# Eight tokens' gate one-hots per VectorE pass, 37 leading key rows and gate runs of 384 bytes in a product-key expert layer

## The chip, the cores and the metric

One NeuronCore of one Trainium2 chip runs the whole program. The metric is the device time of one execution in microseconds (us). The engines that matter here are TensorE (PE, with its weight loads PEld), VectorE (DVE), ScalarE (ACT), GpSimd (POOL) and SyncE (SP), which only issues DMAs here.

## What is computed

Two transformer blocks on 512 tokens of width 1024. The first mixes by a gated delta rule and a forgetting attention, with a SwiGLU layer; the second has a windowed attention, a short convolution and the layer that the change touches, `peer`. It picks for each token, by 8 heads, 16 of 16384 experts and adds up their outputs:

```python
def peer(h, wq, subkeys, u_tab, v_tab):
    q = (xt @ wq).reshape(T, PEER_HEADS, 2, PEER_HALF)
    sc = jnp.einsum('thpd,hpkd->thpk', q, subkeys)
    vals, ids = lax.top_k(sc, PEER_TOPK)
    cand = (vals[:, :, 0, :, None] + vals[:, :, 1, None, :]).reshape(T, PEER_HEADS, 256)
    cid = (ids[:, :, 0, :, None] * PEER_KEYS + ids[:, :, 1, None, :]).reshape(T, PEER_HEADS, 256)
    top, pos = lax.top_k(cand, PEER_TOPK)
    idx = jnp.take_along_axis(cid, pos, axis=-1)
    g = jax.nn.softmax(top, axis=-1)
    ...
        a = jnp.einsum('chkd,cd->chk', jnp.take(u_tab, ic, axis=0), xc)
        wgt = gc * jax.nn.gelu(a)
        return jnp.einsum('chk,chkd->cd', wgt, jnp.take(v_tab, ic, axis=0))
```

An expert's number is 128 times a first key (0 to 127) plus a second key (0 to 127).

## The kernel before

The tokens lie in four tiles of 128. For tiles 1 to 3 (384 tokens, `ND`) the layer is computed densely: all 16384 experts' products with the 384 tokens, times a gate that is zero for the experts not picked. For tile 0 the picked rows of the two tables are fetched by indirect DMAs (`gather`), multiplied on DVE, and added up.

**The dense part** goes by first keys r, 128 of them, each with 128 experts. `ustep` makes the 128x384 products of row r (24 matmuls with 384 columns: the fp32 operands are each split in a high and a low part, and three of the four products are taken, eight times over the width) and ACT writes their gelu into a ring of rows X (`xrow`). `vstep` multiplies a row by its gates (`gmul`), splits it (`eh` on ACT, `el` on DVE in `split`), and adds it times the second table into six PSUM banks (18 matmuls with 512 columns). The weights of either step come as 512 KB loads into three buffers `wraw` (`wdma`, on SP's queue) and are split into `whi` (ACT, L232) and `wlo` (DVE, L234 in this part).

**The gates** of the dense part form a 128x128 matrix for each token (first key by second key). `gates_of` makes it on PE: for a token, a one-hot of the second keys of its 128 picks (`o2`, 128 picks by 128 keys, in fp16) and a one-hot of the first keys scaled by the gate's high and low part (`wh`, `wl`), then two matmuls with 128 columns. Before the change it takes 4 tokens at a time: 12 DVE instructions with 128 columns (L1969 to L1971), then 8 matmuls into one PSUM bank (`sums`), one ACT pass (L1959) that writes it into the staging tile `sg` of 12 tokens (two buffers), and, when that is full, one DMA from ACT's queue (L1963) of 768 KB into the tensor G in HBM. The sums stand one step behind the one-hots. G is read back by first keys in groups of `GR` rows (`ring`, L1829, on SP's queue, two buffers `gt`).

**The order** is written by hand with generators. `chosen` (the top 16 of a tile's candidates and their keys, on DVE), `weigh` (the softmax) and `gates_of` yield costs; `tick(pace)`, called 8 times in a `ustep` and 8 times in a `vstep`, adds `pace` to an account and runs that work until the account is used up. So the pace sets how much gate work stands between two matmuls of a step. The stages of `peer` are:

1. The last scores' top 16 and the first `ustep`s.
2. `ustep`s up to row `LEAD`, with `chosen` and the gates of tiles 1 to 3 between their matmuls, at `PACE0`. What is left of that work is finished behind the last of these steps. X has NX1 + NX2 row slots, one more than LEAD.
3. Pairs of a `ustep` (row k + LEAD) and a `vstep` (row k): first with `chosen` of tile 0 (`PACE1`), then with the gather (`PACE2`).
4. `vstep`s alone, when all 128 products are made, with what is left of the gather (`PACE3`). `preload` fetches the residual rows into free slots of X, `finish` writes the result.

Of the kernel before, what the change touches and what calls it, by code (L numbers as in the profile page):

```python
# [10 lines left out]
F32 = mybir.dt.float32  # L11
F32R = mybir.dt.float32r
F16 = mybir.dt.float16
I32 = mybir.dt.int32
U32 = mybir.dt.uint32
AF = mybir.ActivationFunctionType
OP = mybir.AluOpType
# [12 lines left out]
ND = 384  # L30
TB = 12
NB = ND // TB
GR = 4
GS = 32768.0

NX1, NX2 = 30, 14
LEAD = 43
NLAST = 18

PACE0, PACE1, PACE2, PACE3 = 0.62, 0.27, 0.21, 0.15  # L40

C_ANW, C_FNW, C_GNW, C_CW, C_AOG, C_COG, C_CW2, C_CT, C_N1, C_N2, C_FIN, C_N = 0, 8, 16, 17, 65, 69, 73, 85, 93, 101, 109, 117
R_ALOG, R_DTB, R_FB, R_SNK, R_QG, R_KG, R_IF, R_N = 0, 4, 8, 16, 24, 88, 152, 184
# [85 lines left out]
class Kern:  # L129
# [1580 lines left out]
    def peer(self):  # L1710


        nc, tc, a = self.nc, self.tc, self.a
        V, S, G = nc.vector, nc.scalar, nc.gpsimd
        hi, lo = self.h2
        with ExitStack() as es:
            qp = es.enter_context(tc.tile_pool(name="qp", bufs=1))
            self.X = [self.tl(qp, [128, NX1, ND], F32)]
            hm = self.tl(qp, [128, D], F32)
            ga = self.tl(qp, [128, D], F32)  # L1720
            self.idx = self.tl(qp, [128, 128], I32)
            self.g0 = self.tl(qp, [128, 128], F32)
            av = self.tl(qp, [128, 128], F32)
            self.i1T, self.i2T, self.ghT, self.glT = [self.tl(qp, [128, ND], F32) for _ in range(4)]
            iota = self.tl(qp, [128, 128], F16)
            self.G = self.tl(self.dr, [128 // GR, 128, NB, GR, TB], F32)
            ub = [self.bank("gx") for _ in range(2)]
            with tc.tile_pool(name="q1", bufs=1, side="right") as q1:
                vals = self.tl(q1, [128, 4, 16, 16], F32)
                ids = self.tl(q1, [128, 4, 16, 16], U32)  # L1730
                with tc.tile_pool(name="q2", bufs=2, side="right") as q2:
                    sub = self.tl(q2, [128, 16, 128], F32, bufs=1)
                    nc.sync.dma_start(sub, a["sub"].rearrange("p (a k) -> p a k", a=16))

                    def second(f, qT):
                        p2 = self.bank("pj")
                        for t in range(4):
                            g = slice(t * 128, t * 128 + 128)
                            self.mm(p2[:, g], qT[:, g], sub[:, f])
                        sc = self.tl(q2, [128, 4, 128], F32, "sc")  # L1740
                        S.copy(sc, p2.rearrange("p (t k) -> p t k", t=4))
                        self.top16(*[[x[:, t] for t in range(4)] for x in (sc, vals[:, :, f], ids[:, :, f])])
                    pend = []
                    for f in range(16):
                        p = self.first[f][0] if f < 3 else self.proj512(hi, lo, 0)
                        qT = self.tl(q2, [128, T], F32, "qT", bufs=5)
                        S.copy(qT, p)
                        if f == 3:

                            for n in range(2):  # L1750
                                pb = self.bank("pj")
                                for j in range(4):
                                    k = n * 4 + j
                                    t0 = self.tl(q2, [128, 128], F32, "t0")
                                    V.tensor_tensor(t0, hi.bitcast(F32)[:, k, 0:128], lo.bitcast(F32)[:, k, 0:128], op=OP.add)
                                    self.tr(pb[:, j * 128:j * 128 + 128], t0)
                                S.copy(hm[:, n * 512:n * 512 + 512], pb)
                        pend.append((f, qT))
                        if f > 2:
                            second(*pend.pop(0))  # L1760
                        if f == 4:
                            self.topk_consts(q1, iota)
                    for n, x in enumerate(pend):
                        second(*x)
                        if n < len(pend) - 1:
                            self.ustep(hi, lo, n, ub)
                    r0 = len(pend) - 1
                xp = es.enter_context(tc.tile_pool(name="xp", bufs=1, reuse_waits="tile"))
                self.X.append(self.tl(xp, [128, NX2, ND], F32))
                self.due = 0.0  # L1770
                gp = tc.tile_pool(name="q3", bufs=1, side="right", reuse_waits="tile")
                q3 = gp.__enter__()
                work = self.choice(q1, q3, vals, ids, iota)

                def tick(pace):
                    self.due += pace
                    while self.due > 0:
                        c = next(work, None)
                        self.due = self.due - c if c else -1e9
                for r in range(r0, LEAD):  # L1780
                    self.ustep(hi, lo, r, ub, lambda: tick(PACE0))
                for _ in work:
                    pass
                gp.__exit__(None, None, None)
                self.due = 0.0

                rp = es.enter_context(tc.tile_pool(name="rp", bufs=2, reuse_waits="tile"))
                self.ring(rp, 0)
                last = self.chosen(q1, 0, vals[:, 0], ids[:, 0])
                vb = [self.bank("gx")] + [self.bank("pj") for _ in range(4)] + [self.bank("hold")]  # L1790
                gat = self.gather(qp, hm, ga, av)

                def rest():
                    yield from last
                    for x in self.late:
                        yield from x
                    self.chose0 = True
                    yield from gat
                work = rest()
                self.gmul(rp, 0)  # L1800
                self.split(rp, 0)

                k = 0
                self.chose0 = False
                while not self.chose0:
                    self.ustep(hi, lo, LEAD + k, ub, lambda: tick(PACE1))
                    self.vstep(rp, k, vb, lambda: tick(PACE1))
                    k += 1
            for k in range(k, 126):
                if k + LEAD < 128:  # L1810
                    self.ustep(hi, lo, LEAD + k, ub, lambda: tick(PACE2))
                pace = PACE2 if k + LEAD < 128 else PACE3
                self.vstep(rp, k, vb, lambda: tick(pace))
                if k == 128 - NLAST:
                    self.preload()
            for _ in work:
                pass
            self.finish(rp, ga, vb)
# [126 lines left out]
    def gates_of(self, q3, t, iota):  # L1945

        nc, V, S = self.nc, self.nc.vector, self.nc.scalar
        lag = []

        def sums(n, o2, wh, wl):  # L1950
# [10 lines left out]
            if q + 4 == TB:  # L1961
                b = n * 4 // TB
                nc.scalar.dma_start(self.G[:, :, b].rearrange("g p r t -> p g (r t)"),  # L1963
                                    self.stage.rearrange("p (g r) t -> p g (r t)", r=GR))
        for n in range((t - 1) * 32, t * 32):
            o2, wh, wl = [self.tl(q3, [128, 4, 128], F16, tag, bufs=2) for tag in ("o2", "wh", "wl")]
            for j in range(4):
                c = slice(n * 4 + j, n * 4 + j + 1)
                V.tensor_scalar(o2[:, j], iota, self.i2T[:, c], None, op0=OP.is_equal)  # L1969
                V.tensor_scalar(wh[:, j], iota, self.i1T[:, c], self.ghT[:, c], op0=OP.is_equal, op1=OP.mult)  # L1970
                V.tensor_scalar(wl[:, j], iota, self.i1T[:, c], self.glT[:, c], op0=OP.is_equal, op1=OP.mult)  # L1971
            lag.append((n, o2, wh, wl))
            yield 0.6
            if len(lag) > 1:
                sums(*lag.pop(0))
            yield 0.6
        sums(*lag.pop(0))

    def gather(self, qp, hm, ga, av):
        nc, a = self.nc, self.a  # L1980
# [142 lines left out]
    def weigh(self, q1, t, tv, i1, i2):  # L2123
        nc = self.nc
        V, S = nc.vector, nc.scalar
        tt = lambda shape, dt, tag, n=1: self.tl(q1, shape, dt, "c" + tag, bufs=n)
# [11 lines left out]
        o = slice((t - 1) * 128, t * 128)  # L2138
        pt = self.bank("pj")
        for n, v in enumerate((i1, i2, g)):  # L2140
            self.tr(pt[:, n * 128:n * 128 + 128], v)
        S.copy(self.i1T[:, o], pt[:, 0:128])
        S.copy(self.i2T[:, o], pt[:, 128:256])
        gh = tt([128, 128], F16, "gh")
        S.activation(gh, pt[:, 256:384], AF.Copy, scale=GS)
        S.copy(self.ghT[:, o], gh)
        V.scalar_tensor_tensor(self.glT[:, o], pt[:, 256:384], GS, gh, op0=OP.mult, op1=OP.subtract)
        yield 0.3


# [12 lines left out]
```

## Time and profile before

| | us |
|---|---|
| median of 3 runs | 2482.51 (2479.33 to 2485.78) |
| the profiled execution | 2484.06 |
| its span | 2482.2 |
| PE busy in the span | 2350.2 (95%) |
| DVE busy | 1746.3 (70%) |
| ACT busy | 899.8 (36%) |

The span runs from the first to the last instruction of the program; the profiled execution's own time is 1.9 us longer, and 1.55 us above the median. A row of the profile names a line of the kernel, an engine, an operation and the tiles (output <- inputs); a busy time is the sum of durations, and neighbouring instructions of one engine overlap a little, so that starts tell more than durations where instructions are short. `u` is the name of every tile without one: the rows X, the key tiles, the accumulator of the gather. [...]

### The profile page before, as it was taken

What the parts mean: (1) busy time and instruction counts of PE and PEld (TensorE: products, weight loads), DVE (VectorE), ACT (ScalarE), POOL (GpSimd) and SP (SyncE); (2) the same over time, 40 slices, a digit from 0 to 9 for tenths busy, and PEclk for the clock granted to TensorE, in tenths of its full rate; (3) what the DMA queues carried; (4) which work ended last, traced back from release to release, by engine and by line L of the source; (5) the groups of instructions that cost most, each with busy time, mean ns of one, the idle gap of its engine ahead of it and who ended that gap; (6) DMA issues with size and microseconds to landing.
All of it is one profiled execution on the core that took longest, in us unless ns stands there. A gap on an engine that the chain in (4) does not pass through costs nothing. (4 is left out here: it accounts for less than half of the span.)

```text
span 2482.2 us, 32865 instructions
## 1 busy us (share of the span) xinstructions
PE 2350.2 (95%) x12063; PEld 1978.1 (80%) x12063; DVE 1746.3 (70%) x3991; ACT 899.8 (36%) x1389; POOL 795.1 (32%) x519
## 2 busy tenths in 40 slices
PE   7898999999999999989888888899999999999998
PEld 7888778877778777778767666789999999998776
DVE  6875334465540356757999999677878887878776
ACT  4442423332222333343335454343333333333332
POOL 3553102455544443433000000033434343434221
PEclk9899878999999999999989888999999999999999
DMA  3122000365552221232256677589999899999885
GB/s 120 57 76 76 26 1 11 126 232 193 203 153 93 77 85 59 69 111 86 77 116 131 132 137 138 147 286 319 336 323 329 321 337 321 335 326 324 280 319 174
DMA packets 254493, 438.13 MB, mean 177 GB/s; under 512 B 155006, under 2 KB 155926, under 8 KB 254204
## 3 DMA queue, kind: packets, MB, share of 16 engines
q1 hardware_dynamic: 84476, 272.79, 31.7%
q0 software_dynamic: 37312, 135.20, 15.8%
q10 hardware_dynamic: 132544, 28.05, 7.0%
q8 instruction: 94, 1.54, 0.3%
q14 instruction: 67, 0.55, 0.1%
HBM read 405.22 MB, written 30.70 MB: 176 GB/s over the span
## 5 line engine op out<-in xcount | busy, mean ns | idle before, releaser
L232 ACT CAST whi<-wraw 128x1024 fp32r<-128x1024 f32 x400 | 418.7, 1048 | 327.3 <-issue 125.1
L234 POOL TENSOR_TENSOR wlo<-wraw,whi 128x1024 fp32r<-128x1024 f32 x135 | 353.0, 2616 | 381.9 <-ACT whi L232 377.7
L234 DVE TENSOR_TENSOR wlo<-wraw,whi 128x1024 fp32r<-128x1024 f32 x265 | 329.6, 1244 | 160.1 <-ACT whi L232 158.1
L1996 POOL DMA_INDIRECT gr<-in_pu_dram,u x128 | 153.3, 1198 | 673.4 <-DVE u L2119 447.2
L161 PE MATMUL gx<-alo,whi 128*128 128x384 f32 x1024 | 353.6, 345 | 0.0
L161 PE MATMUL gx<-ahi,whi 128*128 128x384 f32 x1024 | 353.6, 345 | 0.0
L161 PE MATMUL pj<-ahi,whi 128*128 128x512 f32 (+2 forms) x1000 | 322.2, 362 | 3.4 <-ACT ahi L339 3.1
L161 PE MATMUL pj<-alo,whi 128*128 128x512 f32 (+2 forms) x1000 | 314.3, 354 | 0.0
L1996 POOL DMA_INDIRECT gr<-in_pv_dram,u x128 | 152.1, 1188 | 279.4 <-DVE u L2015 209.9
L161 PE MATMUL gx<-ahi,wlo 128*128 128x384 f32 x1024 | 219.8, 355 | 11.8 <-DVE wlo L234 11.8
L161 PE MATMUL pj<-ahi,wlo 128*128 128x512 f32 (+2 forms) x1000 | 211.2, 355 | 2.2 <-DVE wlo L234 2.2
L161 PEld LDWEIGHTS pj<-ahi,whi 128*128 128x128 f32 x1000 | 176.5, 194 | 35.9 <-issue 7.5
L161 PEld LDWEIGHTS gx<-ahi,whi 128*128 128x128 f32 x1024 | 197.1, 192 | 7.7
L161 PEld LDWEIGHTS gx<-alo,whi 128*128 128x128 f32 x1024 | 196.9, 192 | 6.9
L161 PEld LDWEIGHTS gx<-ahi,wlo 128*128 128x128 f32 x1024 | 188.9, 199 | 16.8 <-DVE wlo L234 15.0
L161 PE MATMUL pj<-whi,eh 128*128 128x512 f32 x512 | 201.4, 393 | 0.0
L161 PE MATMUL pj<-wlo,eh 128*128 128x512 f32 x512 | 200.6, 392 | 0.0
L161 PEld LDWEIGHTS pj<-alo,whi 128*128 128x128 f32 x1000 | 176.0, 193 | 23.8
L161 PEld LDWEIGHTS pj<-ahi,wlo 128*128 128x128 f32 x1000 | 166.3, 193 | 29.0 <-DVE wlo L234 2.6
L161 PE MATMUL pj<-whi,el 128*128 128x512 f32 x512 | 180.1, 392 | 0.0
L1899 ACT ACTIVATE u<-gx 128x384 f32<-128x384 f32 x128 | 63.4, 495 | 302.2 <-PE gx L161 294.9
L2015 DVE SCALAR_TENSOR_TENSOR u<-gr,u,u 128x1024 f32<-128x1024 f32 x128 | 163.8, 1280 | 3.2 <-DMA gr<-in_pv_dram,u 2.4
(472 smaller groups left out, 4152.4 us busy)
## 6 DMA issues: line engine op xcount, KB each, us to landing
wraw<-in_put_dram SPq DMA_DIRECT2D x128, 512.0 KB
wraw<-in_pv_dram SPq DMA_DIRECT2D x128, 512.0 KB
nu<-in_adaw_dram SPq DMA_DIRECT2D x48, 512.0 KB
u<-sg ACTq DMA_DIRECT2D x32, 768.0 KB
gt<-u SPq DMA_DIRECT2D x32, 768.0 KB
wraw<-in_wgu_dram SPq DMA_DIRECT2D x44, 512.0 KB
wraw<-in_wi_dram SPq DMA_DIRECT2D x28, 512.0 KB
wraw<-in_wd_dram SPq DMA_DIRECT2D x22, 512.0 KB
```

What stands on the lines that cost most here:

```text
L161: self.nc.tensor.matmul(out, l, r, start=start, stop=stop)
L232: self.nc.scalar.copy(hi, raw)
L234: (self.nc.vector if i in self.lov else self.nc.gpsimd).tensor_tensor(lo, raw, hi.bitcast(F32), op=OP.subtract)
L1899: self.nc.scalar.activation(self.xrow(r), p, AF.Gelu_apprx_tanh)
L1996: G.indirect_dma_start(out=u, out_offset=None, in_=a[items[i][0]], in_offset=bass.IndirectOffsetOnAxis(ap=self.idx[:, items[i][1]:items[i] ...
L2015: V.scalar_tensor_tensor(ga, u, wv[:, s:s + 1], ga, op0=OP.mult, op1=OP.add)
```

## The change

`gates_of` takes 8 tokens at a time, with four DVE instructions of 1024 columns: both operands are tiles read with a broadcast. For that the keys and gates of the 384 tokens (`i1T`, `i2T`, `ghT`, `glT`) are kept as fp16, each value twice side by side, so that the innermost run of every operand is two neighbouring elements. `wh` is first the bare one-hot; `wl` is made from it, then it is scaled in place. The sums of the step before come in two halves. `GR` is 8: G is laid out in groups of 8 first keys, so a run in HBM has 8 x 12 x 4 = 384 bytes (192 before), and a read fetches 8 rows (1.5 MB). X has 38 slots and LEAD is 37. When the gates are done before row LEAD, the tiles of the later stages are opened there and the rest of the `ustep`s run with `chosen` of tile 0 at `PACE1`.

```diff
-GR = 4
+GR = 8
-NX1, NX2 = 30, 14
-LEAD = 43
-NLAST = 18
-PACE0, PACE1, PACE2, PACE3 = 0.62, 0.27, 0.21, 0.15
+NX1, NX2 = 30, 8
+LEAD = 37
+NLAST = 11
+PACE0, PACE1, PACE2, PACE3 = 0.85, 0.27, 0.21, 0.15
...
-            self.i1T, self.i2T, self.ghT, self.glT = [self.tl(qp, [128, ND], F32) for _ in range(4)]
+            self.i1T, self.i2T, self.ghT, self.glT = [self.tl(qp, [128, ND, 2], F16) for _ in range(4)]
...
                 for r in range(r0, LEAD):
-                    self.ustep(hi, lo, r, ub, lambda: tick(PACE0))
-                for _ in work:
-                    pass
-                gp.__exit__(None, None, None)
...
+                    self.ustep(hi, lo, r, ub, lambda: tick(PACE0 if not ready else PACE1))
+                    if r == LEAD - 1:
+                        for _ in range(0 if ready else 10**6):
+                            if next(work, None) is None:
+                                break
+                    if not ready and (self.due < -1e6 or r == LEAD - 1):
+                        ready = True
+                        gp.__exit__(None, None, None)
+                        self.due = 0.0
+                        rp = es.enter_context(tc.tile_pool(name="rp", bufs=2, reuse_waits="tile"))
+                        self.ring(rp, 0)
+                        gat = self.gather(qp, hm, ga, av)
...
+                        work = rest()
...
-            for j in range(4):
-                c = slice(n * 4 + j, n * 4 + j + 1)
-                V.tensor_scalar(o2[:, j], iota, self.i2T[:, c], None, op0=OP.is_equal)
-                V.tensor_scalar(wh[:, j], iota, self.i1T[:, c], self.ghT[:, c], op0=OP.is_equal, op1=OP.mult)
-                V.tensor_scalar(wl[:, j], iota, self.i1T[:, c], self.glT[:, c], op0=OP.is_equal, op1=OP.mult)
...
+            bt = lambda ap: ap[:, n * GT:n * GT + GT].unsqueeze(2).to_broadcast([128, GT, 64, 2])
+            V.tensor_tensor(v4(o2), b2, bt(self.i2T), op=OP.is_equal)
+            yield 0.66
+            V.tensor_tensor(v4(wh), b2, bt(self.i1T), op=OP.is_equal)
+            yield 0.66
+            V.tensor_tensor(v4(wl), v4(wh), bt(self.glT), op=OP.mult)
+            yield 0.66
+            V.tensor_tensor(v4(wh), v4(wh), bt(self.ghT), op=OP.mult)
             lag.append((n, o2, wh, wl))
...
+            for m in range(2 if len(lag) > 1 else 0):
+                sums(lag[0][0] * 2 + m, *[x[:, m * 4:m * 4 + 4] for x in lag[0][1:]])
```

On DVE, in the gates of tile 1 before the change (`o` is `o2`, 128x128 its size; `u_8624` and `u_8623` are the keys, `u_8625` and `u_8626` the gates' parts):

```order
L1969 TENSOR_SCALAR o_1840_10306<-u_8627,u_8624 128x128
L1970 TENSOR_SCALAR wh_10307<-u_8627,u_8623,u_8625 128x128
L1971 TENSOR_SCALAR wl_10308<-u_8627,u_8623,u_8626 128x128
L1969 TENSOR_SCALAR o_1845_10338<-u_8627,u_8624 128x128
L1970 TENSOR_SCALAR wh_10339<-u_8627,u_8623,u_8625 128x128
L1971 TENSOR_SCALAR wl_10340<-u_8627,u_8623,u_8626 128x128
```

And at that place after the change, with one split of weights (`wlo`) among three steps of 8 tokens:

```order
L1974 TENSOR_TENSOR o_1883_10511<-u_8627,u_8624 128x1024
L1976 TENSOR_TENSOR wh_10512<-u_8627,u_8623 128x1024
L234 TENSOR_TENSOR wlo_10522<-wraw_10320,whi_10520 128x1024
L1978 TENSOR_TENSOR wl_10513<-wh_10512,u_8626 128x1024
L1980 TENSOR_TENSOR wh_10512<-wh_10512,u_8625 128x1024
L1974 TENSOR_TENSOR o_1892_10559<-u_8627,u_8624 128x1024
L1976 TENSOR_TENSOR wh_10560<-u_8627,u_8623 128x1024
L1978 TENSOR_TENSOR wl_10561<-wh_10560,u_8626 128x1024
L1980 TENSOR_TENSOR wh_10560<-wh_10560,u_8625 128x1024
L1974 TENSOR_TENSOR o_1897_10596<-u_8627,u_8624 128x1024
```

Four long instructions stand where 24 short ones stood, and two of the four read what the one before them or the second before them wrote.

On ACT, at the end of the gates before the change (L1899 is the gelu that ends a `ustep`, L1836 the `eh` that begins a `vstep`):

```order
L1959 ACTIVATE sg_13618<-pj_13648 128x4x128
L1959 ACTIVATE sg_13618<-pj_13661 128x4x128
L1963 DMA u_8628<-sg_13618 128x32x48
L1899 ACTIVATE u_9635<-gx_8630 128x384
L232 CAST whi_13691<-wraw_13509 128x1024
L1899 ACTIVATE u_9635<-gx_8629 128x384
L1836 CAST eh_13735<-u_8617 128x384
```

And after it:

```order
L1962 ACTIVATE sg_12263<-pj_12275 128x4x128
L1966 DMA u_8628<-sg_12263 128x16x96
L1902 ACTIVATE u_9635<-gx_8629 128x384
L232 CAST whi_12308<-wraw_12115 128x1024
L1902 ACTIVATE u_9635<-gx_8630 128x384
L232 CAST whi_12352<-wraw_12230 128x1024
L1902 ACTIVATE u_9635<-gx_8629 128x384
L232 CAST whi_12405<-wraw_12312 128x1024
L1902 ACTIVATE u_9635<-gx_8630 128x384
L232 CAST whi_12436<-wraw_12356 128x1024
L1902 ACTIVATE u_9635<-gx_8629 128x384
L1839 CAST eh_12494<-u_8617 128x384
```

Two gelus stood between the last store of gates and the first `vstep`, now five do, and the stored pieces are 16 groups of 96 values in place of 32 of 48.

On SP, the first loads of gate rows before the change (`put` is the first table, `pv` the second):

```order
L221 DMA wraw_13643<-in_pv_dram 128x1024
L221 DMA wraw_13695<-in_put_dram 128x1024
L1829 DMA gt_13726<-u_8628 128x1536
L221 DMA wraw_13743<-in_pv_dram 128x1024
L221 DMA wraw_13792<-in_put_dram 128x1024
L221 DMA wraw_13838<-in_pv_dram 128x1024
L1829 DMA gt_13865<-u_8628 128x1536
```

And after it:

```order
L221 DMA wraw_12115<-in_put_dram 128x1024
L221 DMA wraw_12230<-in_put_dram 128x1024
L1832 DMA gt_12306<-u_8628 128x3072
L221 DMA wraw_12312<-in_put_dram 128x1024
L221 DMA wraw_12356<-in_put_dram 128x1024
L221 DMA wraw_12409<-in_pv_dram 128x1024
L221 DMA wraw_12440<-in_put_dram 128x1024
L221 DMA wraw_12502<-in_pv_dram 128x1024
L221 DMA wraw_12538<-in_put_dram 128x1024
L221 DMA wraw_12573<-in_pv_dram 128x1024
L1832 DMA gt_12600<-u_8628 128x3072
```

The first load of gate rows now stands ahead of weights of the first table, and each is twice as large.

## Rows read from the trace of the kernel before

**Rows 1.** Windows by stage: length, then PE, PEld, DVE, ACT, POOL busy, PEclk, DMA, GB/s.
```profile
1189.80:1263.60 73.80, 57.37 (x304) 54.15 (x302) 72.43 (x335) 22.12 (x33) 0.00 (x0) 0.95 0.26 86
1263.60:1351.70 88.10, 76.66 (x431) 55.78 (x431) 85.87 (x391) 44.46 (x47) 0.00 (x0) 0.87 0.69 133
1351.70:1381.70 30.00, 25.83 (x147) 25.02 (x146) 29.28 (x122) 16.36 (x23) 0.00 (x0) 1.00 0.42 102
1381.70:1560.40 178.70, 154.87 (x877) 112.22 (x878) 174.59 (x789) 89.31 (x97) 0.00 (x0) 0.89 0.78 140
...
1568.10:2279.30 711.20, 704.84 (x3553) 641.78 (x3553) 571.97 (x799) 252.87 (x349) 268.36 (x221) 1.00 0.87 312
2279.30:2482.20 202.90, 191.93 (x792) 145.16 (x790) 151.31 (x187) 63.93 (x88) 42.50 (x40) 1.00 0.76 263
```
**Rows 2.** Waits, 1263.6 to 1560.4: who waited for whom, us, times, longest.
```profile
PEld L161 <- DVE o L1969: 39.2, 138, 0.3
PE pj L161 <- DVE wh L1970: 38.9, 132, 5.4
```
**Rows 3.** Timeline of DVE in the gates: start, us, instruction; one token.
```profile
1382.34 0.25 DVE L1969 TENSOR_SCALAR o<-u,u 128x128 f16<-128x128 f16 x1
...
1382.94 0.25 DVE L1969 TENSOR_SCALAR o<-u,u 128x128 f16<-128x128 f16 x1
```
**Rows 4.** Timeline of DVE in chosen, fp16 tensor by tensor, then a weight split.
```profile
1257.70 1.22 DVE L2112 TENSOR_TENSOR ccmp<-cpos,u 128x2048 f16<-128x2048 f16 x1
1258.96 1.71 DVE L2089 TENSOR_TENSOR cmu<-ccmp,cdl 128x256 f16<-128x256 f16 x8
1260.70 1.47 DVE L2094 TENSOR_TENSOR cmu<-cmu 128x1024 f16<-128x1024 f16 x3
1262.21 0.29 DVE L2096 TENSOR_TENSOR ci<-cmu 128x128 f32<-128x128 f16 x1
1262.42 1.22 DVE L234 TENSOR_TENSOR wlo<-wraw,whi 128x1024 fp32r<-128x1024 f32 x1
1263.55 0.25 DVE L1969 TENSOR_SCALAR o<-u,u 128x128 f16<-128x128 f16 x1
```
**Rows 5.** Groups of DVE by form, 1195 to 1600: busy us, mean ns.
```profile
L2094 DVE TENSOR_TENSOR cmu<-cmu 128x1024 f16<-128x1024 f16 x9 | 6.2, 692 | 0.3
L2062 DVE TENSOR_TENSOR cdl<-cidf 128x960 f16<-128x960 f16 x4 | 4.6, 1152 | 0.0
```
**Rows 6.** Timeline of PE in the gates, matmuls with 128 columns back to back.
```profile
1406.44 0.23 PE L161 MATMUL pj<-wh,o 128*128 128x128 f16 x1
...
1406.73 0.22 PE L161 MATMUL pj<-wl,o 128*128 128x128 f16 x1
```
**Rows 7.** Timeline of ACT: the gelu of successive ustep, alone, then in pairs.
```profile
1563.94 0.49 ACT L1899 ACTIVATE u<-gx 128x384 f32<-128x384 f32 x1 [2.09 <-PE gx L161]
...
1568.13 0.49 ACT L1899 ACTIVATE u<-gx 128x384 f32<-128x384 f32 x1 [2.76 <-PE gx L161]
...
1690.45 0.49 ACT L1899 ACTIVATE u<-gx 128x384 f32<-128x384 f32 x1 [3.10 <-PE gx L161]
...
1698.74 0.49 ACT L1899 ACTIVATE u<-gx 128x384 f32<-128x384 f32 x1 [3.09 <-PE gx L161]
```
**Rows 8.** Groups of ACT, 1381.7 to 1560.4: busy us, mean ns, idle before.
```profile
L1959 ACT ACTIVATE sg<-pj 128x512 f32<-128x512 f32 x63 | 69.3, 1100 | 87.9 <-PE pj L161 87.4
```
**Rows 9.** The page's DMA queues: packets, MB, share of 16 engines' span.
```profile
q10 hardware_dynamic: 132544, 28.05, 7.0%
```
**Rows 10.** Timeline of DVE in vstep alone, with the gather's L2015.
```profile
2439.35 1.22 DVE L234 TENSOR_TENSOR wlo<-wraw,whi 128x1024 fp32r<-128x1024 f32 x1 [0.39 <-ACT whi L232]
2440.49 1.28 DVE L2015 SCALAR_TENSOR_TENSOR u<-gr,u,u 128x1024 f32<-128x1024 f32 x1
2441.68 0.55 DVE L1834 TENSOR_TENSOR u<-u,gt 128x384 f32<-128x384 f32 x1
...
2443.84 1.23 DVE L234 TENSOR_TENSOR wlo<-wraw,whi 128x1024 fp32r<-128x1024 f32 x1 [0.39 <-ACT whi L232]
```

More of the change, by code (lines that the diff above doesn't have):

```diff
@@ L1779, in tick, with rest @@
                         self.due = self.due - c if c else -1e9
+                self.chose0 = False
+                ready = False
                 for r in range(r0, LEAD):
-                    self.ustep(hi, lo, r, ub, lambda: tick(PACE0))
-                for _ in work:
-                    pass
-                gp.__exit__(None, None, None)
[L1785 to L1789, printed above, removed]
-                vb = [self.bank("gx")] + [self.bank("pj") for _ in range(4)] + [self.bank("hold")]
[L1791 to L1799, printed above, removed]
+                    self.ustep(hi, lo, r, ub, lambda: tick(PACE0 if not ready else PACE1))
[10 more added lines that the diff above has]
+                        gat = self.gather(qp, hm, ga, av)
+                        def rest():
+                            yield from self.chosen(q1, 0, vals[:, 0], ids[:, 0])
+                            for x in self.late:
+                                yield from x
+                            self.chose0 = True
+                            yield from gat
+                        work = rest()
+                vb = [self.bank("gx")] + [self.bank("pj") for _ in range(4)] + [self.bank("hold")]
                 self.gmul(rp, 0)
@@ L1803, in peer @@
                 k = 0
-                self.chose0 = False
                 while not self.chose0:
@@ L1964, in sums @@
                                     self.stage.rearrange("p (g r) t -> p g (r t)", r=GR))
-        for n in range((t - 1) * 32, t * 32):
-            o2, wh, wl = [self.tl(q3, [128, 4, 128], F16, tag, bufs=2) for tag in ("o2", "wh", "wl")]
-            for j in range(4):
-                c = slice(n * 4 + j, n * 4 + j + 1)
-                V.tensor_scalar(o2[:, j], iota, self.i2T[:, c], None, op0=OP.is_equal)
-                V.tensor_scalar(wh[:, j], iota, self.i1T[:, c], self.ghT[:, c], op0=OP.is_equal, op1=OP.mult)
-                V.tensor_scalar(wl[:, j], iota, self.i1T[:, c], self.glT[:, c], op0=OP.is_equal, op1=OP.mult)
+        GT = 8
+        b2 = iota.rearrange("p (a b) -> p a b", b=2).unsqueeze(1).to_broadcast([128, GT, 64, 2])
+        v4 = lambda ap: ap.rearrange("p t (a b) -> p t a b", b=2)
+        for n in range((t - 1) * 16, t * 16):
+            o2, wh, wl = [self.tl(q3, [128, GT, 128], F16, tag, bufs=2) for tag in ("o2", "wh", "wl")]
+            bt = lambda ap: ap[:, n * GT:n * GT + GT].unsqueeze(2).to_broadcast([128, GT, 64, 2])
[6 more added lines that the diff above has]
+            V.tensor_tensor(v4(wh), v4(wh), bt(self.ghT), op=OP.mult)
             lag.append((n, o2, wh, wl))
-            yield 0.6
+            for m in range(2 if len(lag) > 1 else 0):
+                sums(lag[0][0] * 2 + m, *[x[:, m * 4:m * 4 + 4] for x in lag[0][1:]])
+                if m == 0:
+                    yield 0.66
             if len(lag) > 1:
-                sums(*lag.pop(0))
-            yield 0.6
-        sums(*lag.pop(0))
+                lag.pop(0)
+            else:
+                yield 0.66
+        for m in range(2):
+            sums(lag[0][0] * 2 + m, *[x[:, m * 4:m * 4 + 4] for x in lag[0][1:]])
     def gather(self, qp, hm, ga, av):
@@ L2141, in weigh @@
             self.tr(pt[:, n * 128:n * 128 + 128], v)
[L2142 to L2147, printed above, removed]
+        two = lambda k: pt[:, k * 128:k * 128 + 128].unsqueeze(2).to_broadcast([128, 128, 2])
+        S.copy(self.i1T[:, o], two(0))
+        S.copy(self.i2T[:, o], two(1))
+        S.activation(self.ghT[:, o], two(2), AF.Copy, scale=GS)
+        V.scalar_tensor_tensor(self.glT[:, o], two(2), GS, self.ghT[:, o], op0=OP.mult, op1=OP.subtract)
         yield 0.3
```

## The prediction, made before the changed kernel ran

> **What bounds the kernel now.** Read the windows by stage first [rows 1]. They cut the expert layer, 1189.8 to 2482.2 us, into the last top 16 with `chosen` of tiles 1 and 2 (73.8 us), the gates of tile 1 (88.1), `chosen` of tile 3 (30.0), the gates of tiles 2 and 3 (178.7), a tail of two `ustep`s from 1560.4 to 1568.1 (7.7), the pairs (711.2) and the `vstep`s alone (202.9). In the pairs PE is busy for 704.84 of 711.2 us at a granted clock of 1.00: that stage is PE's, and nothing that DVE saves there counts. Up to 1560.4 it is the other way round. [...]
>
> So the gates run at DVE's rate. One token costs 0.60 us there from one `o2` to the next [rows 3], though each of its three instructions has only 128 columns. 384 tokens make 230 of the 266.8 us of the two gate windows; weight splits, 1.13 us each [rows 4], make most of the rest.
>
> What PE needs for the same work is little. A `ustep` by itself takes 4.19 us from gelu to gelu [rows 7], or 0.175 us for each of its 24 matmuls; a matmul of the gates 0.058 (0.29 for five) [rows 6], so 0.93 for 8 tokens.
>
> **The one-hots.** Removed: 24 instructions, 4.80 us, for 8 tokens. Added: four of 1024 columns. No row shows their operand shape (runs of two, broadcast between), so the price comes from fp16 tensor-by-tensor neighbours. The 2048 columns of L2112, whose reader follows at once, take 1.26 us from start to start; eight of 256 columns take 1.74, 0.22 each; 1024, 512 and 256 columns, each reading the one before, take 1.51 together [rows 4]. Two prices fit these: 0.52 ns a column, and 0.19 us for an instruction whose result the next one waits for, 0.08 for others. So 1024 columns cost 0.73 or 0.61; the nearest row has 692 ns of duration [rows 5], between them. Two of the four are read at once by the next (`wh` by `wl`, `wl` by the in-place scaling's wait): 2 x 0.61 + 2 x 0.73 = 2.68 us. The other end is 1.13 us, what 1024 columns cost where a pass moves one element at a time, as the fp32 weight split does [rows 4], and 960 fp16 columns with a repeated innermost element do too, at 1152 ns [rows 5]. I take 2.68, since the innermost run is two different elements, as in L2089's runs of four, which go at the fast price.
>
> [...]
>
> **The gate stages.** A `ustep` calls tick 8 times at 0.85, and 8 tokens yield 4 x 0.66, so 2.58 groups of 8 stand in one `ustep`. A group costs DVE 2.68 + 1.13/2.58 = 3.12 us, PE 0.93 + 4.19/2.58 = 2.55 at the full clock, and ACT at most 2.79 (89.31 us for 32 groups' worth [rows 1]; two staging passes of 1.10 us are most of it, and ACT now idles behind PE [rows 8]). All three now lie close, and they are tied: `o2` of a group waits until PE has summed the group before the last (two buffers), and PE's sums wait for DVE. [...] PE will pause less than now, but what it pauses now is mostly hidden. I take 3.5, near the second, and for the range 3.15 to 4.0 (the second plus waits for the staging tile, below). 48 groups: 168 us for 266.8, **98 less** (81 to 115).
>
> The other windows shrink a little, since at 0.85 fewer `ustep`s and their splits stand in them: by the changed order 10 gelus before the first staged gates, 12 before, and one less in `chosen` of tile 3: 3 x 1.13, **3 less**. Behind the gates five `ustep`s now run where the tail had two: 5 x 4.19 + 3 against 7.7, **16 more**. `chosen` of tile 0 under them costs nothing, since a `ustep` there leaves DVE 4.19 us for a split (1.13) and 2.16 of paced work; without PE as the bound it would add about 3 us each.
>
> **What LEAD moves.** Six fewer `ustep`s lead, so there are 91 pairs, not 85, at 8.29 us [rows 7]: **50 more**. Six `vstep`s fewer run alone, at 4.49 (2439.35 to 2443.84) [rows 10]: **27 less**. The 711.2 us hold 85 x 8.29 = 704.7 and 6.5 of waiting at the start, for the first gate rows and for `chosen`; with five `ustep`s in between, **4 less**. More pairs also take in more of the gather: by the order its last 17 `vstep`s-alone instructions stand where 39 did, so 16 more `vstep`s run without one. With it DVE's chain sets the 4.49, and 1.19 of that is the gather's (2440.49 to 2441.68) [rows 10]; without, the chain would be 3.3, and PE's 8.29 - 4.19 = 4.10 is late next. 16 x 0.39: **6 less**.
>
> **Gate rows.** 16 loads of 1.5 MB replace 32 of 0.75. DMA is 87% busy in the pairs at 312 GB/s [rows 1], the weights behind a load on SP's queue come up to 0.75 MB / 312 GB/s = 2.4 us later, and there are 11 such places in the pairs. Three `wraw` buffers hide most of it. From 0 to 27; I take **3 more**. The stores halve their runs: 132544 packets of the queue took 7.0% of 16 x 2482.2 us [rows 9], 21 ns each; at the same price for a packet a 768 KB store falls from 5.4 us to 2.7. It has to land within two staging periods of 4.7 us (1.5 groups), so it is hidden; with an unchanged 5.4 plus issue it just is.
>
> **The sum.** -98 - 3 + 16 + 50 - 27 - 4 - 6 + 3 = -69. The span goes from 2482.2 to 2413, the execution from 2484.06 to 2415; that execution lies 1.55 above the median, so I predict **2413 us**. Gate groups at 3.15 and no late weights give 2393, at 4.0 with 12 us of late weights 2446.
>
> **Rivals.** *One element at a time.* If DVE doesn't pair elements in runs of two, an instruction costs 1.13 or 1.25, a group 4.76 + 0.44 = 5.20, with 5% for waits 5.45, and 48 groups 262 us. That is 94 more: **2507**, slower than now. It decides from 4.95 a group (3.5 + 69/48) or 1.03 us an instruction. For it: L2062, and that no row has this shape. Against: L2089. [...]
>
> *Late weights.* The 1.5 MB loads leave PE without weights at each of the 11 places for 2.4 us, and a few times behind: 30 more, **2440**. For it: 87% of DMA busy. Against: an average load that doesn't change.
>
> *Stores.* Runs of 384 bytes may cost by the byte, as much again as two of 192, so a store keeps its 5.4 us of all 16 engines and comes twice as often. Twelve tokens are 1.5 groups, or 0.58 of a `ustep`, with a weight load of 512 KB at 312 GB/s, 1.68 us. DMA then needs 5.4 + 0.58 x 1.68 = 6.4 us for 12 tokens and sets the rate: 32 x 6.4 = 205 us, 37 more, **2450**. For it: DMA is busy at 0.78 in the gates already. Against: 192 bytes in 21 ns are 9 GB/s for an engine, under half of the 312/16 = 19.5 in the pairs, so most of the 21 ns goes by the packet. [...]
>
> **How the numbers follow.** The forecast, 2390 to 2430, has 0.68; late weights 0.09; stores 0.08; one element at a time 0.10; a mix of losses that leaves the time within 0.3% (about 7 us, what a measurement can tell from no change) 0.03; below 2390, with an unthrottled PE, 0.02. The range 2390 to 2450 holds the first three, stores at its edge. Faster by over 0.3%: 0.87, the same 0.03, slower 0.10.
>
> **What would show it.** The four new lines at 0.61 to 0.73 us from start to start (not 1.13); the two gate windows 168 us long in all, not 267; a granted clock of 0.85 to 0.95 there; the gelu of row 36 near 1482 and 757 us from there to the last; 8.29 us a pair also behind a load of gate rows, and 4.1 us a `vstep` at the end. I am wrong if the new lines cost over 1 us, if ACT waits for a store at each third pass, or if pairs stretch every eighth time.

## The result and the profile after

The changed kernel takes 2409.51 us (median of four, 2407.29 to 2410.73); the kernel before took 2481.68 in the same comparison. The ratio is 0.9706, 95% interval 0.9690 to 0.9723: 72 us faster. The profiled execution took 2407.29 us, with a span of 2405.5.

The same stages as in [rows 1], of the kernel after. Columns: stretch and length, then PE, PEld, DVE, ACT and POOL busy, PEclk (the granted clock as a share of full speed), DMA share, GB/s.

```profile
1182.90:1253.60 70.70, 47.58 (x245) 44.65 (x243) 69.30 (x332) 19.31 (x28) 0.00 (x0) 0.89 0.21 67
1253.60:1312.70 59.10, 45.37 (x372) 39.32 (x372) 48.56 (x72) 37.53 (x40) 0.00 (x0) 0.87 0.65 181
1312.70:1343.00 30.30, 21.59 (x125) 20.47 (x125) 26.97 (x118) 15.92 (x22) 0.00 (x0) 0.91 0.33 99
1343.00:1467.40 124.40, 93.97 (x789) 82.08 (x789) 99.19 (x146) 80.43 (x89) 0.00 (x0) 0.90 0.65 179
1467.40:1489.40 22.00, 21.98 (x128) 21.98 (x129) 11.78 (x63) 7.82 (x10) 0.00 (x0) 0.93 0.72 235
1489.40:2242.90 753.50, 751.46 (x3806) 685.21 (x3805) 613.14 (x797) 271.61 (x375) 294.35 (x244) 1.00 0.89 320
2242.90:2405.50 162.60, 155.45 (x684) 127.89 (x682) 110.35 (x138) 56.13 (x75) 20.80 (x17) 0.99 0.62 220
```

The gates, second and fourth row, fell from 266.8 to 183.5 us. The `ustep`s (products) behind them take 22.0 for 7.7, the pairs 753.5 for 711.2, the `vstep`s alone 162.6 for 202.9. From the first row to the end that is 1222.6 us for 1292.4: **69.8 less, where the sum said 69.** The other 6.9 us of the two spans lie ahead of the first row, in code that is the same. That start moves from run to run: it lies between 1176.2 and 1190.0 us in the traces of this study. So below the stages are compared, not only the whole times.

The one-hots in the gates after (DVE's timeline: start, us, instruction):

```profile
1257.95 0.69 DVE L1976 TENSOR_TENSOR wh<-u,u 128x1024 f16<-128x1024 f16 x1
1258.67 0.69 DVE L1978 TENSOR_TENSOR wl<-wh,u 128x1024 f16<-128x1024 f16 x1
1259.40 0.69 DVE L1980 TENSOR_TENSOR wh<-wh,u 128x1024 f16<-128x1024 f16 x1
1260.01 0.69 DVE L1974 TENSOR_TENSOR o<-u,u 128x1024 f16<-128x1024 f16 x1
1260.61 0.68 DVE L1976 TENSOR_TENSOR wh<-u,u 128x1024 f16<-128x1024 f16 x1
```

From start to start 0.72, 0.73, 0.61 and 0.60 us: 2.66 for 8 tokens, where 24 instructions took 4.80 [rows 3].

Yet DVE is no longer busy all the time: 48.56 of 59.10 us and 99.19 of 124.40, about 80% where it was 97 to 98% [rows 1]. Who waits in the gates after (1253.6 to 1467.4; us in total, times, longest):

```profile
ACT sg L1962 <- PE pj L161: 43.3, 30, 10.9
DVE wlo L234 <- ACT whi L232: 32.7, 18, 4.7
ACT sg L1962 <- DMA u<-sg: 21.3, 9, 3.8
DVE o L1974 <- PE pj L161: 2.5, 4, 0.9
```

Before, DVE waited for `whi` 6.3 us in these stretches. In the two gate stretches alone it is now 30.2 us, and DVE waits for PE only 2.5. How the second and the third row hang together shows in ACT's timeline (in brackets the idle time ahead of an instruction and who ended it):

```profile
1387.06 0.39 ACTq L1966 DMA_DIRECT2D u<-sg  x1
1387.56 3.12 ACT L1962 ACTIVATE sg<-pj 128x512 f32<-128x512 f32 x3 [0.53 <-ACT sg L1962]
1390.70 0.37 ACTq L1966 DMA_DIRECT2D u<-sg  x1
1394.33 1.99 ACT L1962 ACTIVATE sg<-pj 128x512 f32<-128x512 f32 x2 [3.66 <-DMA u<-sg]
1396.13 0.52 ACT L1902 ACTIVATE u<-gx 128x384 f32<-128x384 f32 x1
1396.55 1.02 ACT L232 CAST whi<-wraw 128x1024 fp32r<-128x1024 f32 x1
```

The store issued at 1387.06 still reads its staging tile when, at 1390.70, the other tile is full. ACT stands for 3.66 us before it can write the first one again, 7.27 us after the store's issue (6.1 to 8.2 in the nine waits), and the cast of the next weights, `whi`, is queued behind that. DVE's split needs `whi`, and the one-hots are queued behind the split.

### The profile page after: what moved, and what is told of

Read it like the earlier page. It is cut to its first block, busy times and chain, and to the rows that moved or that the text cites. A ratio compares the mean times of both kernels' runs of the same rounds, so it can differ in the third digit from the quotient of the medians.

```text
span 2405.5 us, 31911 instructions
## 1 busy us (share of the span) xinstructions
PE 2257.5 (94%) x12063; PEld 1948.3 (81%) x12063; DVE 1639.1 (68%) x3031; ACT 897.0 (37%) x1386; POOL 800.8 (33%) x519
## 4 chain that ended last, share of the span: by engine, by line
PE 74%; DVE 15%; ACT 5%; DMA 3%; issue 2%; POOL 1%; SPq 0%; ACTq 0%; DVEq 0%; POOLq 0%
PE pj L161 42%; PE gx L161 25%; PE hold L161 5%; DMA u<-sg 2%; PE gx L185 2%; DVE w L634 2%; DVE wlo L234 1%; ACT whi L232 1%; ACT sg L1962 1%; DVE w L768 1%; DVE cmu L2108 1%; DVE cmu L2103 0%; DMA wraw<-in_wi_dram 0%; POOL alo L343 0%; DVE w L632 0%
## 5 line engine op out<-in xcount | busy, mean ns | idle before, releaser
L2010 POOL DMA_INDIRECT gr<-in_pv_dram,u x128 | 157.7, 1232 | 233.3 <-DVE u L2029 174.0
L161 PE MATMUL gx<-ahi,wlo 128*128 128x384 f32 x1024 | 214.2, 349 | 18.9 <-DVE wlo L234 18.9
L2029 DVE SCALAR_TENSOR_TENSOR u<-gr,u,u 128x1024 f32<-128x1024 f32 x128 | 163.9, 1281 | 2.5 <-DMA gr<-in_pv_dram,u 1.6
```

The costliest lines, as they stand in the source:

```text
L161: self.nc.tensor.matmul(out, l, r, start=start, stop=stop)
L2010: G.indirect_dma_start(out=u, out_offset=None, in_=a[items[i][0]], in_offset=bass.IndirectOffsetOnAxis(ap=self.idx[:, items[i][1]:items[i] ...
L2029: V.scalar_tensor_tensor(ga, u, wv[:, s:s + 1], ga, op0=OP.mult, op1=OP.add)
```

## The experiments

Stages in us, from the profiled run of each. "Gates" is both stretches, "behind" the products between the last one-hot and the first pair. The gates of after, e6_lead33 and e9_phase do the same work and lie 2.7 us apart, so a difference of under 3 us there tells nothing. The first four expectations count from 178 us of gates in the changed kernel; by the same cut as the other rows it is 183.5.

| kernel | median, ratio to before (95%) | gates | behind | pairs | alone |
|---|---|---|---|---|---|
| before | 2481.68 | 266.8 | 7.7 | 711.2 | 202.9 |
| after | 2409.51, 0.9706 (0.9690–0.9723) | 183.5 | 22.0 | 753.5 | 162.6 |
| e1_single | 2474.99, 0.9983 (0.9972–0.9994) | 251.3 | 22.7 | 753.5 | 162.6 |
| e2_old | 2476.55, 0.9991 (0.9979–1.0002) | 256.5 | 21.6 | 753.6 | 162.6 |
| e3_sg3 | 2390.58, 0.9635 (0.9609–0.9660) | 163.3 | 22.2 | 753.6 | 162.6 |
| e4_pool | 2395.15, 0.9668 (0.9637–0.9700) | 168.4 | 24.4 | 752.7 | 162.6 |
| e5_gr4 | 2419.59, 0.9756 (0.9725–0.9787) | 196.7 | 22.2 | 753.4 | 162.6 |
| e6_lead33 | 2422.68, 0.9768 (0.9731–0.9804) | 180.9 | 6.6 | 794.2 | 150.4 |
| e7_sg3_pace76 | 2401.29, 0.9691 (0.9657–0.9726) | 172.1 | 7.4 | 762.1 | 171.0 |
| e8_sg3_late | 2385.89, 0.9623 (0.9592–0.9655) | 163.9 | 21.9 | 753.0 | 162.6 |
| e9_phase | 2417.81, 0.9732 (0.9706–0.9757) | 180.8 | 22.0 | 753.4 | 168.7 |
| e10_sg3_gr4 | 2400.84, 0.9679 (0.9653–0.9705) | 177.5 | 22.2 | 753.5 | 162.6 |
| e11_before_phase | 2466.31, 0.9943 (0.9922–0.9964) | 267.3 | 7.7 | 711.1 | 189.9 |

**Is it the run of two?**

```diff
-        b2 = iota.rearrange("p (a b) -> p a b", b=2).unsqueeze(1).to_broadcast([128, GT, 64, 2])
+        b2 = iota.unsqueeze(1).to_broadcast([128, GT, 128])
-        v4 = lambda ap: ap.rearrange("p t (a b) -> p t a b", b=2)
+        v4 = lambda ap: ap
-            bt = lambda ap: ap[:, n * GT:n * GT + GT].unsqueeze(2).to_broadcast([128, GT, 64, 2])
+            bt = lambda ap: ap[:, n * GT:n * GT + GT, 0:1].to_broadcast([128, GT, 128])
```

> The changed kernel, but the four one-hot instructions read the token's value with a repeated innermost element and the key numbers in one run of 128, so no operand has the innermost run of two. Theory (the run of two is what makes a pass go at 0.52 ns a column): an instruction costs 1.13 us from start to start, 1.25 where the next one reads its result, 4.76 for 8 tokens; with 1.13/2.58 of a weight split 5.20 a group, with waits up to 5.45; 48 groups 250 to 262 us for 178 in the changed kernel: 2481 to 2493 us. Rival (a broadcast operand goes at the fast price anyway): 0.61 and 0.73 as in the changed kernel, 2409 us.

2474.99 us, and DVE's timeline in its gates:

```profile
1253.76 1.22 DVE L1976 TENSOR_TENSOR wh<-u,u 128x1024 f16<-128x1024 f16 x1
1255.01 1.22 DVE L1978 TENSOR_TENSOR wl<-wh,u 128x1024 f16<-128x1024 f16 x1
1256.27 1.22 DVE L1980 TENSOR_TENSOR wh<-wh,u 128x1024 f16<-128x1024 f16 x1
1257.41 1.22 DVE L1974 TENSOR_TENSOR o<-u,u 128x1024 f16<-128x1024 f16 x1
1258.55 1.22 DVE L234 TENSOR_TENSOR wlo<-wraw,whi 128x1024 fp32r<-128x1024 f32 x1
```

1.25, 1.26, 1.14 and 1.14 us from start to start, the prediction's 1.13 and 1.25. The gates take 251.3 / 48 = 5.24 us a group, what the prediction's first rival has (5.20) without its 5% of waits. They lie in the theory's 250 to 262 us; the time lies 6 us under its range, which starts from the 178. The theory stands, and it says more: eight tokens in one instruction gain next to nothing by themselves. With a repeated innermost element four long instructions take 4.79 us where 24 short ones took 4.80, and 68 us of the gates sit in the inner run of two.

**The one-hots undone.** The old 24 instructions in everything else that is new (`...` marks lines left out; the keys and gates are kept as fp32 again for it):

```diff
-            V.tensor_tensor(v4(o2), b2, bt(self.i2T), op=OP.is_equal)
...
-            V.tensor_tensor(v4(wh), b2, bt(self.i1T), op=OP.is_equal)
...
-            V.tensor_tensor(v4(wl), v4(wh), bt(self.glT), op=OP.mult)
...
-            V.tensor_tensor(v4(wh), v4(wh), bt(self.ghT), op=OP.mult)
+            for j in range(8):
+                if j in (2, 4, 6):
+                    yield 0.66
+                c = slice(n * 8 + j, n * 8 + j + 1)
+                V.tensor_scalar(o2[:, j], iota, self.i2T[:, c], None, op0=OP.is_equal)
+                V.tensor_scalar(wh[:, j], iota, self.i1T[:, c], self.ghT[:, c], op0=OP.is_equal, op1=OP.mult)
+                V.tensor_scalar(wl[:, j], iota, self.i1T[:, c], self.glT[:, c], op0=OP.is_equal, op1=OP.mult)
```

> The changed kernel with the old 24 one-hot instructions for 8 tokens; LEAD 37, pace 0.85, runs of 384 bytes and 1.5 MB loads stay. Theory (the gain is the one-hots'): a group costs DVE 4.80 + 1.13/2.58 = 5.24 us, with the waits of the kernel before 5.56; 48 groups 251 to 267 us for 178: 2482 to 2498 us, so the rest of the change is worth between nothing and 16 us lost. Rival (LEAD, larger runs and fewer stores carry a part): under 2465 us.

2476.55 us, gates 256.5: the gates lie in the theory's 251 to 267 us, the time between its range and the rival's. So 73 us of gates hang on the one-hots, and without them LEAD, pace, runs and loads together can't be told from the kernel before (0.9979 to 1.0002).

**A third staging tile.**

```diff
-                self.stage = self.tl(q3, [128, 128, TB], F32, "sg", bufs=2)
+                self.stage = self.tl(q3, [128, 128, TB], F32, "sg", bufs=3)
```

> The changed kernel with three staging tiles in place of two. Theory (what the gates take above DVE's own work is ACT waiting for a store, 21 us in nine waits, and with it whi and wlo late): these waits go, the gate windows fall from 178 to about 160 us, 2390 to 2398 us. Rival (the wait only moves: ACT or DVE would next wait for PE's sums at a reduced clock): gates 172 to 178 us, 2403 to 2410 us.

2390.58 us, the theory's number. No wait of ACT for a store is left in its gates, and DVE's wait for `whi` has shrunk (1258.9 to 1451.6):

```profile
ACT sg L1962 <- PE pj L161: 41.2, 35, 10.9
DVE wlo L234 <- ACT whi L232: 13.1, 14, 1.7
```

The gates take 163.3 us, 3.40 a group: 20 us of the changed kernel's 183.5 hung on this wait. This version beats both kernels: its ratio of 0.9635 stands against the changed kernel's 0.9706.

**The splits on POOL.** POOL has no work in the gates, so it could take what DVE waits with:

```diff
-        self.lov.update(range(n, len(w)))
+        self.lov.update(range(n + LEAD, len(w)))
```

> The changed kernel with the weight splits of the 37 leading products on POOL, which has no instruction between 1182.9 and 1461 us. Theory (the stages up to the end of the gates go at DVE's rate and DVE's waits are those for whi ahead of a split): a group costs DVE 2.65 us, ACT 2.79 and PE 2.55 at the full clock, so 2.9 to 3.3 with waits, 48 groups 139 to 158 us for 178; ten splits fewer in the first window of chosen and four in chosen of tile 3, 16 us: 2355 to 2375 us. Rival (the split of 2.62 us on POOL stretches beside DVE's passes and PE waits for it instead): the windows stay, 2400 to 2415 us.

2395.15 us, between what the theory and what the rival said: the gates are 15 us shorter than in the changed kernel, not 25 to 45, and the 16 us in the windows of `chosen` did not come at all (71.3 and 31.8 us for 70.7 and 30.3, though ten and five splits ran on POOL there). Two groups of DVE in its gates (1254 to 1452; busy us, mean ns, idle before):

```profile
L1974 DVE TENSOR_TENSOR o<-u,u 128x1024 f16<-128x1024 f16 x47 | 49.6, 1056 | 3.6 <-PE pj L161 3.5
L1976 DVE TENSOR_TENSOR wh<-u,u 128x1024 f16<-128x1024 f16 x47 | 40.9, 870 | 0.0
```

One place in the timelines of POOL and DVE:

```profile
1390.11 2.56 POOL L234 TENSOR_TENSOR wlo<-wraw,whi 128x1024 fp32r<-128x1024 f32 x1 [10.37 <-ACT whi L232]
...
1390.34 2.88 DVE L1974 TENSOR_TENSOR o<-u,u 128x1024 f16<-128x1024 f16 x1
```

The `o2` that starts beside a split on POOL takes 2.88 us in place of 0.69: it ends at 1393.22, 0.55 us after that split (1392.67). Over the group `o2` rises from 685 to 1056 ns, `wh` to 870, the other two from 691 to 780: 47 x 0.73 = 34 us, more than the 21 splits of 1.13 (24 us) that left DVE. What is won is that DVE no longer waits for `whi`. What holds DVE up beside POOL the trace does not name.

**Runs of 192 bytes.**

```diff
-GR = 8
+GR = 4
```

> The changed kernel with runs of 192 bytes (GR 4): the same bytes in twice the packets, 32 loads of 0.75 MB in place of 16 of 1.5 MB in the pairs. Theory (a store costs by the packet, and it is the staging tile's wait for it that the gates feel, 21 us in the changed kernel): the wait grows by 10 to 30 us, the pairs stay at 8.29 us: 2416 to 2436 us. Rival (a store costs by the byte, or its cost is hidden): 2403 to 2411 us. If large loads made weights late, the pairs would get faster here: under 2403 us.

2419.59 us, at the theory's lower end. ACT's wait for a store grew from 21.3 to 39.1 us (16 times), the gates from 183.5 to 196.7. The pairs stayed at 753.4: loads of 1.5 MB cost them nothing. And with three staging tiles:

> Three staging tiles and runs of 192 bytes. Theory (the run's length reaches the time only through ACT's wait for a staging tile, so a third tile hides it): gates as with three tiles and 384 bytes, pairs 2 us shorter as with two tiles and 192 bytes, 2386 to 2392 us. Rival (the stores' rate itself is the bound once their latency is hidden, with twice the packets): 2395 to 2410 us.

2400.84 us: the rival. No pass of ACT waits for a staging tile here, and the gates still take 14 us more than with 384 bytes. ACT now stands in issuing the stores:

```profile
1363.54 3.20 ACTq L1966 DMA_DIRECT2D u<-sg  x1
1366.85 1.08 ACT L1962 ACTIVATE sg<-pj 128x512 f32<-128x512 f32 x1 [3.33 <-PE pj L161]
```

With 384 bytes and three tiles such an issue takes 0.37 us, 12 us for all 32; here the 32 take 26, and that difference is as large as the gates' (the view puts the idle time down to PE). The DMA queues in the gates of the changed kernel, then of this one (packets, MB, share of 16 engines):

```profile
q10 hardware_dynamic: 62355, 23.76, 43.1%
q1 hardware_dynamic: 3312, 12.06, 17.3%
```

```profile
q10 hardware_dynamic: 123512, 23.62, 81.9%
q1 hardware_dynamic: 3312, 12.06, 18.9%
```

The same bytes take nearly twice the engine time: 43.1% of 16 x 213.8 us over 62355 packets is 23.6 ns each, 81.9% of 16 x 206.9 over 123512 is 22.0. With 192 bytes the stores and the weights fill all 16 engines (81.9 + 18.9; the two gate stretches by themselves show 1.07 and 1.11). A share above 1 means that packets overlap on an engine, so 22 and 23.6 ns are how long a packet is under way, not what it costs alone. So a store is paid nearly by the packet, and the longer run gains 13 to 14 us in the changed kernel. In the kernel before, with the same 192 bytes, DMA stood at 0.69 and 0.78 [rows 1] and ACT waited for no store in the gates; the run of 384 was not tried there by itself.

**What LEAD moves.**

```diff
-LEAD = 37
+LEAD = 33
```

> The changed kernel with LEAD 33 in place of 37. Theory (behind the gates a product is worth its 4.19 us, a pair 8.29, a vstep alone 4.08): four products fewer behind the gates, -16.8, four more pairs, +33.2, four vsteps fewer alone, -16.3: +0.1, 2403 to 2411 us. Rival (the products behind the gates cover the way of the last gates through DRAM and chosen of tile 0): without them PE waits there, up to 17 us more, 2415 to 2425 us.

2422.68 us: the rival. The products behind the gates fell by 15.4 us as counted, but the 95 pairs take 794.2, not 95 x 8.29 = 787.6, and at their start stands one wait that the changed kernel doesn't have (1474.4 to 1500; PE itself stands for 5.3 us of it):

```profile
DVE u L1837 <- DMA gt<-u: 14.0, 1, 14.0
```

The first gate rows have to go out to DRAM and come back: the last store is issued at 1470.87, their load at 1475.55, and DVE starts at 1481.71. The five products cover that way; one doesn't. A LEAD above 37 was not tried. Another 4 us lie in the `vstep`s alone (below, e9). The next run puts nearly all products inside the stages that go at DVE's rate:

```diff
-PACE0, PACE1, PACE2, PACE3 = 0.85, 0.27, 0.21, 0.15
+PACE0, PACE1, PACE2, PACE3 = 0.76, 0.27, 0.21, 0.15
```

> Three staging tiles and PACE0 0.76 in place of 0.85, so that three or four more products run inside the DVE stages and as many fewer behind the gates. Against three staging tiles alone (2390.6 us). Theory (DVE is the bound there, a product costs it a split of 1.13 us; behind the gates it costs PE 4.19): 3.5 x (4.19 - 1.13) = 11 us less, 2377 to 2383 us. Rival (DVE is no longer alone the bound: ACT's evictions and PE at its reduced clock take as long): each product costs in the gates what it costs behind them, 2387 to 2394 us.

2401.29 us, 11 more than with three tiles alone, which neither side expected. 14.8 us are saved behind the gates, but the gates grow by 8.8 and the windows of `chosen` by 4.0: three more products cost there nearly what they cost behind, as the rival had it. What neither had are the pairs, 8.5 longer (their start waits 5.4 us for gate rows), and the `vstep`s alone, 8.4 longer (the gather's place, below). That makes 14.9 from the layer's start on; the profiled execution got there 8 us earlier than that of three tiles alone.

**A later split**, on three tiles:

```diff
+SPLIT = 3
...
-        self.prod(p, self.nextw(), (hi, lo), slice(128, 512), 8, do)
+        if r < LEAD - 1:
+            w, left = self.nextw(0), [SPLIT]
+
+            def step():
+                left[0] -= 1
+                if left[0] == 0:
+                    self.wsplit(self.wi + 1)
+                do()
+            self.prod(p, w, (hi, lo), slice(128, 512), 8, step)
+        else:
+            self.prod(p, self.nextw(), (hi, lo), slice(128, 512), 8, do)
```

> Three staging tiles, and a leading product splits the next product's weights after three eighths of its own matmuls, not ahead of them. Against three staging tiles alone (2390.6 us). Theory (the 20 us that DVE still waits for whi in the gates are casts queued on ACT behind evictions and behind PE's release of the buffer; asked for later, they are there): 10 to 20 us less, 2371 to 2381 us. Rival (DVE then waits for PE to release o2, or PE for the split): 2386 to 2394 us.

2385.89 us, but the gates take 163.9 us for 163.3, and from the first one-hot to the end the two kernels differ by 0.5 us; the profiled executions differ by where the layer starts (1179.1 for 1188.3). No effect: DVE still waits 15.5 us for `whi`.

**The `vstep`s alone.** In the changed kernel nearly every one of them takes 4.08 us, also those with a gather; before, a gathered one took 4.49. DVE's timeline after, to be read beside [rows 10]:

```profile
2260.36 1.23 DVE L234 TENSOR_TENSOR wlo<-wraw,whi 128x1024 fp32r<-128x1024 f32 x1 [0.43 <-ACT whi L232]
2261.50 0.55 DVE L1837 TENSOR_TENSOR u<-u,gt 128x384 f32<-128x384 f32 x1
2261.97 1.28 DVE L2029 SCALAR_TENSOR_TENSOR u<-gr,u,u 128x1024 f32<-128x1024 f32 x1
2263.44 0.56 DVE L1843 TENSOR_TENSOR el<-u,eh 128x384 fp32r<-128x384 f32 x1 [0.20 <-ACT eh L1839]
2264.44 1.23 DVE L234 TENSOR_TENSOR wlo<-wraw,whi 128x1024 fp32r<-128x1024 f32 x1 [0.43 <-ACT whi L232]
```

The gather's pass (L2029) stands behind the multiplication by the gates (L1837), where DVE would wait for `eh` in any case; before, it stood ahead of it [rows 10]. The pacing account happens to stand elsewhere when this stage begins. To move it back, and in the kernel before to move it forward (with `+= 0.3`):

```diff
+                if k + LEAD == 128:
+                    self.due -= 0.6
```

> The changed kernel with 0.6 taken off the paced work's account once, where the vsteps alone begin. The gather's pass then stands between wlo and the multiplication by the gates (as in the kernel before), not between that multiplication and el. Theory (the gather's place decides whether a vstep alone takes 4.49 or 4.08 us): the last 16 or 17 gathered steps take 4.49, 17 x 0.41 = 7 us more behind the last product, 2410 to 2416 us. Rival (it is the number of gathers that counts, or the loads): 4.08 a step also here, 2403 to 2409 us.

> The kernel before with 0.3 added to the paced work's account once, where its vsteps alone begin; the gather's pass then stands between the multiplication by the gates and el, as in the changed kernel. Theory (part of what the changed kernel gained behind the last product is this place, not the smaller number of gathers there): its 38 gathered steps fall from 4.49 to 4.08 us, 38 x 0.41 = 15 us less, 2464 to 2469 us. Rival (with the gather in each step DMA or POOL keep the step at 4.4 to 4.5): 2478 to 2484 us.

Both as the theory had it, by the stage: it takes 168.7 us for 162.6 (steps of 4.50), and in the kernel before 189.9 for 202.9, which makes that kernel 0.57% faster with nothing else changed. The time of the first, 2417.81 us, lies 2 us over its range, but in its profiled execution the layer also starts 7 us later than in the changed kernel's (1190.0 for 1182.9).

## Why the prediction was right

The forecast was 2413 us with 69 less in the layer; 2409.51 and 69.8 came. The direction and its cause, the price of the one-hots, were right; that the sum came so close is in part luck. Step by step:

- **One-hots, 2.68 us for 8 tokens:** 2.66. The fast price, its condition (an innermost run of two) and the choice between the two ends held: 0.60 to 0.73 us from start to start in the trace after, and 1.14 to 1.26 in e1, with one element repeated.
- **Gate groups at 3.5 us, 98 less: mis-sized.** They took 183.5 / 48 = 3.82, 83 less, near the upper end of 4.0 (which stands for 75 less, not the 81 of the prediction: 266.8 - 48 x 4.0); the gelu of row 36 came 306.5 us after the layer's start where 292 was said. The step that failed is "it has to land within two staging periods of 4.7 us, so it is hidden", with 2.7 us for a store. With two tiles a store has one period, not two: the tile is wanted again as soon as the other one is full. And in the nine waits ACT got the tile 6.1 to 8.2 us after the issue; 2.7 is what the packets take of 16 engines, not the whole way, and would have fitted into one period. e3 shows it: 20 us go with a third tile. What 3.5 has over 3.12, 0.38 us for groups slowed by PE at a reduced clock, was the author's estimate, and no run shows that term: the clock was as low as said (0.87 and 0.90) and PE paused more than before, not less (busy for 139 of 183.5 us, before for 232 of 266.8), but of the 33.7 us over 48 x 3.12 DVE waited 2.5 for PE and 30.2 for `whi`, and with three tiles, at 0.89 and 0.95, a group takes 3.40. Whether the low clock delays `whi` by way of ACT, which waits 43.3 us for PE's sums, no run separates.
- **Other windows, 3 less:** 70.7 for 73.8, and 30.3 for 30.0. **Behind the gates, 16 more:** 14.3.
- **Pairs, +50 - 4 + 3:** 42.3 more in all. 91 x 8.29 = 754.4 held to a microsecond (753.5); all 6.5 us of waiting at the start went, not 4, and the late weights cost nothing (e5).
- **`vstep`s alone, -27 - 6:** 40.3 less. With the gather at the old place (e9) it is 34.2 less, so fewer gathered steps were worth what was said. The other 6.1 us are the gather's new place, which the prediction does not have: luck. At that place a gather adds nothing, whatever their number (e11: 13.0 us in the kernel before).
- **Rivals.** One element at a time is the author's name for a price: with a repeated element an instruction costs what was said (1.14 to 1.26 us, e1), and the operands avoid it; how many elements DVE moves at a time no run shows. The rival's 94 us were too many: the gates grow by 67.8, from 183.5 and not from 168, and without the 5% of waits (DVE is busy there for 82.2 of 83.2 and 166.1 of 168.1 us). Late weights: nothing. Stores: by the byte was wrong, 22 to 24 ns a packet came for the 21 taken; but ACT waiting for a store, a sign of being wrong at each third pass, came behind 9 of 32 stores for another reason, the tiles.

So 14.7 us too little in the gates were made up by 1.7, 6.7 and 7.3 behind them, and the total is better than its parts: that is luck. Three tiles leave 3.40 us a group over DVE's 3.12, since DVE still waits 13 us for `whi`; why `whi` is late there stays open, and asking for it later (e8) changed nothing.

## What to carry to other kernels

Before many tokens go into one DVE instruction, look at the innermost run: 1024 fp16 columns cost 0.60 us with runs of two and 1.14 with one element repeated, and only the first was worth a change here. When an engine gets faster, recount each buffer that it feeds by its release: with two buffers a store has one period to land, what counts is the time from issue to release (6.1 to 8.2 us here) and not that of its packets, and the wait is felt on the engine that writes the tile and on all that is queued behind it. And paced side work has a phase: where it lands in a step's chain was worth 0.41 us a step, which any change of a count upstream can give or take.

## What the runs showed that was not expected

A DVE pass of two tensors that started beside a split on POOL ended only after it (2.88 us for 0.69), while the search instructions between the gates kept their mean durations: MAX8 196 ns and FIND_INDEX8 203 to 205, in the changed kernel 198 to 204 and 207 to 212. Packets of 192 and of 384 bytes take almost the same, 22.0 and 23.6 ns, so with the run doubled the stores' share of the 16 engines in the gates fell from 81.9% to 47.8% (e10, e3). And the same code ahead of the layer ended up to 14 us apart from run to run, more than several of the effects measured here, while the stages that PE sets repeated within 1 us (the pairs of all kernels with LEAD 37 and five products behind the gates, 752.7 to 753.6).
